# A dense fill sequence, second low-rank factors one pair earlier, and the RWKV output weights split during the first feed-forward stage

## The chip, the cores and the metric

The kernel runs on one core of one Trainium2 chip. The metric is the device time of one launch, in microseconds (us). The kernel before was run three times; the median is 1318.53 us, the lowest 1314.91 and the highest 1324.61.

A core has five engines that run beside each other, each with its own queue of instructions: PE (TensorE, matrix products), DVE (VectorE), ACT (ScalarE), POOL (GpSimd) and SP (SyncE, which here only starts DMAs). PEld is PE's loading of the stationary operand.

## The reference

The input is one sequence of 512 positions with 1024 channels, float32, and the model has two layers. Each layer adds a token mixer and then a gated feed-forward block to the residual, both behind an RMS norm, and one more RMS norm ends it.

```
layer 0:  h += sgu_mixer(norm(h))          # gated MLP with 128-position causal blocks
          h += conv_ffn(norm(h))           # (silu(gate) * val) @ w_down, FFN_DIM 2816
layer 1:  h += rwkv7_mixer(norm(h))        # 16 heads of 64, state 64x64 per head
          h += conv_ffn(norm(h))
return norm(h)

rwkv7_mixer:  xx = shift(h) - h;  x? = h + xx * mu[?]       for r, w, k, v, a, g
  r, k, v = xr @ w_r, xk @ w_k, xv @ w_v
  w = -softplus(-(w0 + tanh(xw @ w1) @ w2)) - 0.5;   a = sigmoid(a0 + (xa @ a1) @ a2)
  g = sigmoid(xg @ g1) @ g2
  S_t = S_{t-1} diag(exp(-exp(w_t))) + (S_{t-1} a_t) b_t^T + v_t k_t^T ;  y_t = S_t r_t
  return ((group_norm(y) + bonus) * g) @ w_o
```

## The kernel before, in words

**Matrix products.** Activations lie as eight tiles of 128 channels by 512 positions. Every float32 product is made of three fp32r matmuls: each operand is split into a high part (a cast on ACT, L213) and a low part (a subtraction, on DVE or POOL, L214), and `mm3` (L291 to L297) adds high times high, high times low and low times high. A tile of weights is loaded by one DMA from ACT's queue into `w32` (two buffers) and split into `wh` and `wl` (`WB` = 4 buffers each) by `weights`.

**Parts.** Splitting weights costs ACT and DVE time when the weights are used. For `w_k`, `w_v` and the first gate factor `g1`, `make_parts` therefore splits them early, beside the first feed-forward stage (`ffn` with l = 0): a step loads a piece of 128x512 from DRAM (SP, L253), splits the piece of the step before, and writes its two parts back to DRAM (SP, L257). The pieces have two buffers, each part one. In the stage's first loop (22 turns j, each two products of 24 matmuls) one step is taken per turn; in the second loop (8 output tiles) two per tile. With 35 pieces there are 36 steps. Later `parts` and `gate_parts` load the parts directly (L266, L272, L281, L282), with nothing left to split. The output weights `w_o` (`wo`) are not among them: `project` loads and splits them as it uses them, the second half of each load with its low part on POOL.

**The RWKV stage.** `rwkv_first` makes the low-rank hidden layer and r. `rwkv_main` then weaves three generators:

- *main*: `pairs` (eight pairs of heads; `decay`, `operands`, `products`), then two `scan`s over groups of eight heads, each eight chunks of 64 positions. A chunk is a chain in which PE (L1117, L1130, L1137, L1142) and DVE or ACT copies (L1119, L1131, L1132, L1140) wait for each other in turn.
- *side*: `invert`, which inverts the triangular blocks of a group, first on DVE (L964, L965, L970, L971), then with 32x32 matmuls on PE (L985, L988).
- *fill*: one long sequence of dense PE work, `projections` (k, then v; each v tile's `value` work, L784 and L798, is stepped in between as `late`), then `gates` (the gate's two factors), then `project` (the output product).

`weave` (L1258 on) advances main by one yield, adds `rate` to what fill is due, and takes that many steps of fill, whose PE instructions it puts behind the PE mark of `lag` yields earlier. The rates are RATES[0] and [1] for the pairs, [5] for their last two yields, [2] for the first scan, [3] for the second, [4] for the rest. LEAD is the number of fill steps taken between the end of the pairs and the first scan. Apart from such explicit orders the compiler's scheduler orders each engine's queue by its own estimate of when operands are ready.

**Where the changed parts act.** `second_factors` loads the second low-rank factors of two pairs (SP), and splits them (ACT L729, DVE L730) into `l2`, which has one set of buffers; `start` calls it when an even pair begins, and `decay` multiplies with it at once (L814, L816). In `projections`, the last `value` is drained step by step (`yield from late`). `gates` first loads its weights, yields once without PE work, and then per k mixes `x` (ACT L1010, DVE L1011, a split) and multiplies it at once with both columns of `g1`: six matmuls of 512 positions, three of them 32 columns wide. Two steps of the sigmoid follow, without PE work, then four `gate` steps that wait until the first scan's last block is normed. `project` takes two steps of six matmuls for each of 8 output tiles, once per group.

Of the kernel before, what the change touches and what calls it, by code (L numbers as in the profile page):

```python
# [28 lines left out]
GN_EPS = 64e-5  # L29
C1 = -0.5 * math.exp(-0.5)  # L30

RATES = ((1.9, 2), (1.9, 6, 2.2), (0.62, 2, 1), (0.85, 2), (2, 2), (0.7, 6, 2.2))
LEAD = 4
WB = 4
FIRST0, WAIT, STEPS = 1, 1, (2, 2, 2, 2, 2)
NKEY = 3
BT, SCAN = 1, 3
BANKS = ("mm", "aux", "e", "us")
PARTS = ("wk", "wv")


PARAMS = [
# [101 lines left out]
class Emit:  # L144
    def __init__(self, ctx, tc, A, out):
        self.tc, self.nc, self.A, self.out = tc, tc.nc, A, out
        nc = tc.nc
        self.gp = gp = ctx.enter_context(tc.tile_pool(name="gp", bufs=1))
        self.wp = ctx.enter_context(tc.tile_pool(name="wp", bufs=2))

        self.xr = ctx.enter_context(tc.tile_pool(name="xring", bufs=1))
        self.cst = gp.tile([P, NCST], F32, name="cst")
        self.par = gp.tile([P, NPAR], F32, name="par")

        self.hz = [gp.tile([P, T + 1], F32, name=f"h{k}") for k in range(KT)]
# [12 lines left out]

        dp = ctx.enter_context(tc.tile_pool(name="parts", bufs=1, space=DRAM))
        self.wd = {n: [dp.tile([P, 2, 1024], F32, name=f"{n}d{m}") for m in range(KT)] for n in PARTS}  # L170
        self.gd = dp.tile([P, 2, 1280], F32, name="g1d")
        self.n = self.turn = 0
        self.wq = nc.scalar
        self.ktiles = 2
        self.x = []
# [66 lines left out]
    def make_parts(self, pool):  # L242

        nc = self.nc
        at = [(self.A[n][m], self.wd[n][m], slice(c, c + 512)) for n in PARTS for m in range(KT) for c in (0, 512)]
        at += [(self.A["g1"], self.gd, slice(c, min(c + 512, 1280))) for c in (0, 512, 1024)]
        w = []
        for i in range(len(at) + 1):
            with self.tc.issue_after(self.last(mybir.EngineType.Activation)):
                if i < len(at):  # L250
                    src, _, c = at[i]
                    w.append(pool.tile([P, 512], F32, tag="pw", bufs=2, name=self.uid("pw"))[:, 0:c.stop - c.start])
                    nc.sync.dma_start(w[i], src[:, c])  # L253
                if i:
                    _, dst, c = at[i - 1]
                    for j, x in enumerate(self.split(pool, w[i - 1], [P, 512], "pw", bufs=1)):
                        nc.sync.dma_start(dst[:, j, c], x[:, 0:c.stop - c.start].bitcast(F32))  # L257
            yield
# [226 lines left out]
    def ffn(self, l, gain):  # L485
        nc, tc, A = self.nc, self.tc, self.A
        with ExitStack() as ctx:
# [11 lines left out]

            for j in range(NF):  # L500
                cv, accs = [], []
                next(parts, None)
                for i in (j, NF + j):
                    w = self.first if i == 0 else self.weights(A["wup"][l, i])
                    a = self.acc()
                    self.dense(a, w, x)
                    accs.append(a)
                    if i == 0:
                        norm = self.rstd()
                        next(norm)  # L510
# [12 lines left out]
                nc.vector.tensor_tensor(cv[1], cv[0], cv[1], ALU.mult)  # L523
                hid.append(self.split(fp, cv[1], [P, T], f"hid{j}"))
# [169 lines left out]
    def rwkv_main(self, r, ctx, gain):  # L694
# [13 lines left out]
        def tmp(tag, bufs, w=W2):  # L708
            return tile_([P, w], tag, bufs)
# [23 lines left out]
        def projections():  # L733
# [31 lines left out]
            late = iter(())  # L765
            for m in range(KT):
                a = self.acc("mm")
                for _ in self.dense_steps(a, load.take(), xv):
                    yield
                    next(late, None)  # L770
                for _ in late:
                    yield
                v = ip.tile([P, T], F32, tag="v", bufs=1, name=self.uid("v"))
                S.copy(v, a)
                late = value(m, v)
            yield from late

        def value(m, v):
            g, i = divmod(m, 4)
# [29 lines left out]
        def decay(p, u):  # L809
# [4 lines left out]
                nc.tensor.matmul(accs[j], l2[j][:, w], r.lr[j], start=True, stop=False)  # L814
            for j in range(2):
                nc.tensor.matmul(accs[j], l2[2][H[j], w], r.lr[j][H[j]], start=False, stop=True)  # L816
            th, u.ta = scratch("sq"), tmp("ta", 2, T)
            for j, x in enumerate((th, u.ta)):
                S.activation(x, accs[j], AF.Tanh, scale=0.5, bias=dq(j, p))
# [89 lines left out]
        def pairs():  # L909
# [3 lines left out]
            def start(p):  # L913
                if p >= KT:
                    return iter(())
                while p not in ks:
                    next(fill)
                if p % 2 == 0:
                    second_factors(p)
                return decay(p, units[p])  # L920

# [14 lines left out]
        def invert(g):  # L936
# [39 lines left out]
            for i in range(2):  # L976
                for hf in range(2):
# [17 lines left out]
                            S.copy(tg[b0, us, 32:64], ps[b0])  # L995
                    yield

        def gates():


            gw[0] = gate_weights(0)
            ws = self.gate_parts()
            yield
            accs = [self.acc("mm")[0:n] for n in (P, 32)]
            for k in range(KT):
                with ExitStack() as behind:
                    for eng in (mybir.EngineType.DVE, mybir.EngineType.Activation):
                        behind.enter_context(tc.issue_after(self.last(eng)))
                    j, t = 5 * KT + k, scratch("sq")
                    S.activation(t, self.hz[k][:, 0:T], AF.Copy, scale=self.p("mu", j))  # L1010
                    V.scalar_tensor_tensor(t, self.h[k], self.omu[:, j:j + 1], t, ALU.mult, ALU.add)  # L1011
                    x = self.operand(t)
                for a, w, n in zip(accs, ws, (P, 32)):
                    self.mm3(a, self.wcols(w, k * n, n), x, k == 0, k == KT - 1)
                yield
# [170 lines left out]
        def project():  # L1186

            def load(g, m):
                return self.weights(A["wo"][m:m + 2, :, 512 * g:512 * g + 512].rearrange("m p c -> p m c"), lo_eng=G)

            ws = Ahead([lambda g=g, m=m: load(g, m) for g in range(2) for m in range(0, KT, 2)] + [self.prefetch])
            def back(m):
# [128 lines left out]
```

## Time and profile before

| what | us |
|---|---|
| median of three runs | 1318.53 |
| the profiled execution, its own time | 1320.53 |
| its span, first to last instruction | 1318.7 |
| PE busy | 1275.4 |
| DVE busy | 852.3 |
| ACT busy | 631.1 |
| POOL busy | 141.5 |

The mean granted PE clock is 0.974 of full speed. All times of rows below are us from the start of the span. The RWKV stage's `rwkv_main` runs from about 570 to 945, the first scan from 758 to 833, the second until 902. A row of a stretch (A:B) gives each engine's busy time with its number of instructions, then the granted PE clock, the DMA engines' mean busy share, and GB/s. A row of a group gives its count, busy time and the mean nanoseconds of one, then the engine's idle time ahead of it and what ended that. A row of the timeline gives start, duration, the instruction, and in brackets the engine's idle time before it and what ended it.

### The profile page before, as it was taken

What the parts mean: (1) busy time and instruction counts of PE and PEld (TensorE: products, weight loads), DVE (VectorE), ACT (ScalarE), POOL (GpSimd) and SP (SyncE); (2) the same over time, 40 slices, a digit from 0 to 9 for tenths busy, and PEclk for the clock granted to TensorE, in tenths of its full rate; (3) what the DMA queues carried; (4) which work ended last, traced back from release to release, by engine and by line L of the source; (5) the groups of instructions that cost most, each with busy time, mean ns of one, the idle gap of its engine ahead of it and who ended that gap; (6) DMA issues with size and microseconds to landing.
All of it is one profiled execution on the core that took longest, in us unless ns stands there. A gap on an engine that the chain in (4) does not pass through costs nothing. (4 is left out here: it accounts for less than half of the span.)

```text
span 1318.7 us, 19468 instructions
## 1 busy us (share of the span) xinstructions
PE 1275.4 (97%) x7578; PEld 1025.9 (78%) x7578; DVE 852.3 (65%) x1371; ACT 631.1 (48%) x1072; POOL 141.5 (11%) x148
## 2 busy tenths in 40 slices
PE   8999999999999999999999998889999999999996
PEld 6878888888888888777777766567888888888886
DVE  5565487888775443847779584686687777772223
ACT  5444455555554333665675644443554445442221
POOL 3100200000000111211111022142300000000001
PEclk9999999999999999999899896899999999999998
DMA  7232345555556663237778695583322232223322
GB/s 258 89 112 81 109 149 171 167 166 174 170 175 213 218 204 109 81 121 202 204 215 259 165 222 123 128 223 105 96 96 96 96 96 96 96 92 97 95 88 76
DMA packets 101580, 189.06 MB, mean 143 GB/s; under 512 B 17072, under 2 KB 49072, under 8 KB 101488
## 3 DMA queue, kind: packets, MB, share of 16 engines
q10 hardware_dynamic: 36592, 109.46, 26.7%
q1 hardware_dynamic: 64896, 78.37, 20.7%
q8 instruction: 59, 0.97, 0.3%
q14 instruction: 33, 0.27, 0.1%
HBM read 146.63 MB, written 41.16 MB: 142 GB/s over the span
## 5 line engine op out<-in xcount | busy, mean ns | idle before, releaser
L213 ACT CAST wh<-w 128x512 fp32r<-128x512 f32 x356 | 217.0, 612 | 392.3 <-PE mm L296 104.4
L214 DVE TENSOR_TENSOR wl<-w,wh 128x512 fp32r<-128x512 f32 x348 | 239.6, 690 | 184.7 <-ACT wh L213 183.3
L295 PE MATMUL mm<-mxh,wh 128*128 128x512 f32 (+1 forms) x384 | 158.1, 412 | 1.4 <-DVE h L1208 1.3
L297 PE MATMUL mm<-mxh,wl 128*128 128x512 f32 (+1 forms) x384 | 152.7, 398 | 1.6 <-DVE wl L214 1.6
L296 PE MATMUL mm<-mxl,wh 128*128 128x512 f32 (+1 forms) x384 | 152.5, 397 | 0.0
L322 POOL TENSOR_TENSOR ss<-ss,sq 128x512 f32<-128x512 f32 x30 | 41.4, 1379 | 776.8 <-issue 594.8
L518 ACT ACTIVATE cv<-z,par 128x512 f32<-128x512 f32 x88 | 71.7, 817 | 36.1 <-DVE z L516 36.1
L295 PEld LDWEIGHTS mm<-mxh,wh 128*128 128x128 f32 (+1 forms) x384 | 72.7, 189 | 20.7 <-issue 3.4
L297 PEld LDWEIGHTS mm<-mxh,wl 128*128 128x128 f32 (+1 forms) x384 | 72.5, 189 | 19.4 <-DVE wl L214 2.6
L295 PE MATMUL e<-mxh,wh 128*128 128x512 f32 x216 | 84.7, 392 | 0.0
L296 PE MATMUL e<-mxl,wh 128*128 128x512 f32 x216 | 84.3, 390 | 0.0
L297 PE MATMUL e<-mxh,wl 128*128 128x512 f32 x216 | 84.3, 390 | 0.0
L296 PEld LDWEIGHTS mm<-mxl,wh 128*128 128x128 f32 (+1 forms) x384 | 72.9, 190 | 14.5 <-issue 0.5
L296 PE MATMUL aux<-mxl,wh 128*128 128x512 f32 x208 | 81.4, 391 | 1.5 <-POOL mxl L214 1.4
L295 PE MATMUL aux<-mxh,wh 128*128 128x512 f32 x208 | 81.5, 392 | 0.3 <-ACT mxh L213 0.3
L295 PE MATMUL us<-mxh,wh 128*128 128x512 f32 x208 | 81.5, 392 | 0.0
L519 DVE SCALAR_TENSOR_TENSOR cv<-z,par,cv 128x512 f32<-128x512 f32 x88 | 66.0, 751 | 23.9 <-ACT cv L518 23.9
L297 PE MATMUL aux<-mxh,wl 128*128 128x512 f32 x208 | 81.2, 391 | 0.0
L297 PE MATMUL us<-mxh,wl 128*128 128x512 f32 x208 | 81.2, 390 | 0.0
L296 PE MATMUL us<-mxl,wh 128*128 128x512 f32 x208 | 81.2, 390 | 0.0
L520 DVE SCALAR_TENSOR_TENSOR cv<-z,par,cv 128x512 f32<-128x512 f32 x88 | 66.0, 752 | 2.9
L295 PEld LDWEIGHTS e<-mxh,wh 128*128 128x128 f32 x216 | 40.6, 188 | 8.9 <-issue 0.5
(1092 smaller groups left out, 2713.3 us busy)
## 6 DMA issues: line engine op xcount, KB each, us to landing
w<-in_wup ACTq DMA_DIRECT2D x88, 512.0 KB, 3.6
w<-in_wdn ACTq DMA_DIRECT2D x32, 512.0 KB, 3.5
st<-std SPq DMA_DIRECT2D x30, 384.0 KB, 5.4
std<-lq SPq DMA_DIRECT2D x32, 256.0 KB, 4.3
w<-in_wdn ACTq DMA_DIRECT2D x16, 384.0 KB, 3.2
w<-in_wsu ACTq DMA_DIRECT2D x8, 512.0 KB, 3.6
w<-in_wso ACTq DMA_DIRECT2D x8, 512.0 KB, 3.5
pw<-in_wk SPq DMA_DIRECT2D x16, 256.0 KB, 3.7
```

The costliest lines, as they stand in the source:

```text
L213: nc.scalar.copy(hi[r, :n], src)
L214: (lo_eng or nc.vector).tensor_tensor(lo[r, :n], src, hi[r, :n].bitcast(F32), ALU.subtract)
L295: mm(acc, wh, xh, start=first, stop=False)
L296: mm(acc, wh, xl, start=False, stop=False)
L297: mm(acc, wl, xh, start=False, stop=last)
L322: nc.gpsimd.tensor_tensor(self.ss, self.ss, self.sq, ALU.add)
L518: nc.scalar.activation(c, z[:, 2:], AF.Identity, scale=cw(2, i), bias=self.p("conv_b", l * 44 + i))
L519: nc.vector.scalar_tensor_tensor(c, z[:, 1:T + 1], cw(1, i), c, ALU.mult, ALU.add)
L520: nc.vector.scalar_tensor_tensor(c, z[:, 0:T], cw(0, i), c, ALU.mult, ALU.add)
```

## The change

The second factors are made at the end of the odd pair before, gate operands two steps ahead of their use, the gate's weights at the last v tile; two yields of fill without dense work go; `wo` joins the weights split during the first feed-forward stage, with two steps of `make_parts` in each of the first 15 turns; and four rates and LEAD change.

```diff
-RATES = ((1.9, 2), (1.9, 6, 2.2), (0.62, 2, 1), (0.85, 2), (2, 2), (0.7, 6, 2.2))
-LEAD = 4
+RATES = ((1.9, 2), (1.9, 6, 2.2), (0.72, 2, 1), (0.72, 2), (2, 2), (1.2, 6, 2.2))
+LEAD = 1
...
-PARTS = ("wk", "wv")
+PARTS, LATER = ("wk", "wv"), ("wo",)
...
-        at = [(self.A[n][m], self.wd[n][m], slice(c, c + 512)) for n in PARTS for m in range(KT) for c in (0, 512)]
+        at = [(self.A[n][m], self.wd[n][m], slice(c, c + 512)) for n in PARTS + LATER for m in range(KT) for c in (0, 512)]
...
             for j in range(NF):
                 cv, accs = [], []
-                next(parts, None)
+                for _ in range(2 if j < 15 else 1):
+                    next(parts, None)
...
                 a = self.acc("mm")
-                for _ in self.dense_steps(a, load.take(), xv):
+                w = load.take()
+                if m == KT - 1:
+                    gw[0] = gate_weights(0)
+                for _ in self.dense_steps(a, w, xv):
                     yield
                     next(late, None)
+                    if m == KT - 1 and len(gx) < 2:
+                        gx.append(gate_mix(len(gx)))
...
-            yield from late
+            for _ in late:
+                pass
...
                 nc.tensor.matmul(accs[j], l2[2][H[j], w], r.lr[j][H[j]], start=False, stop=True)
+            if p % 2 == 1 and p + 1 < KT:
+                second_factors(p + 1)
...
-                if p % 2 == 0:
+                if p == 0:
                     second_factors(p)
...
+        gx = []
+
+        def gate_mix(k):
+            with ExitStack() as behind:
+                for eng in (mybir.EngineType.DVE, mybir.EngineType.Activation):
+                    behind.enter_context(tc.issue_after(self.last(eng)))
+                j, t = 5 * KT + k, scratch("sq")
+                S.activation(t, self.hz[k][:, 0:T], AF.Copy, scale=self.p("mu", j))
+                V.scalar_tensor_tensor(t, self.h[k], self.omu[:, j:j + 1], t, ALU.mult, ALU.add)
+                return self.operand(t)
+
         def gates():
-            gw[0] = gate_weights(0)
             ws = self.gate_parts()
-            yield
             accs = [self.acc("mm")[0:n] for n in (P, 32)]
             for k in range(KT):
-                with ExitStack() as behind:
...
-                    x = self.operand(t)
+                x = gx[k]
+                if k + 2 < KT:
+                    gx.append(gate_mix(k + 2))
...
             def load(g, m):
-                return self.weights(A["wo"][m:m + 2, :, 512 * g:512 * g + 512].rearrange("m p c -> p m c"), lo_eng=G)
+                t = []
+                for d in self.wd["wo"][m:m + 2]:
+                    x = tuple(self.wp.tile([P, 512], F32R, tag=tag, bufs=WB, name=self.uid(tag)) for tag in ("wh", "wl"))
+                    for i in range(2):
+                        self.wq.dma_start(x[i].bitcast(F32), d[:, i, 512 * g:512 * g + 512])
+                    t.append(x)
+                return 512, t
```

More of the change, by code (lines that the diff above doesn't have):

```diff
@@ L169, in __init__ @@
         dp = ctx.enter_context(tc.tile_pool(name="parts", bufs=1, space=DRAM))
-        self.wd = {n: [dp.tile([P, 2, 1024], F32, name=f"{n}d{m}") for m in range(KT)] for n in PARTS}
+        self.wd = {n: [dp.tile([P, 2, 1024], F32, name=f"{n}d{m}") for m in range(KT)] for n in PARTS + LATER}
         self.gd = dp.tile([P, 2, 1280], F32, name="g1d")
@@ L996, in invert @@
                     yield
+        gx = []
[7 more added lines that the diff above has]
+                return self.operand(t)
         def gates():
-            gw[0] = gate_weights(0)
             ws = self.gate_parts()
-            yield
             accs = [self.acc("mm")[0:n] for n in (P, 32)]
             for k in range(KT):
-                with ExitStack() as behind:
[L1007 to L1011, printed above, removed]
-                    x = self.operand(t)
+                x = gx[k]
+                if k + 2 < KT:
+                    gx.append(gate_mix(k + 2))
                 for a, w, n in zip(accs, ws, (P, 32)):
```

## The prediction

> **What bounds the kernel now.** I read the busy shares first, then the slices of the span, then stretches of the RWKV stage, then single waits of PE in the timeline.
>
> ```profile
> span 1318.7 us, 19468 instructions
> ...
> PE 1275.4 (97%) x7578; PEld 1025.9 (78%) x7578; DVE 852.3 (65%) x1371; ACT 631.1 (48%) x1072; POOL 141.5 (11%) x148
> ...
> PE   8999999999999999999999998889999999999996
> ...
> PEclk9999999999999999999899896899999999999998
> ```
>
> PE bounds the kernel: the other engines are far from full. What the change can return is therefore what PE loses, and both slice rows put that between slices 20 and 27, which is the RWKV stage. PE loses in two ways there: it idles, and its clock is granted at half. Stretches of that stage:
>
> ```profile
> 646.90:657.10 10.20, 10.20 (x56) 8.53 (x57) 5.02 (x10) 6.57 (x12) 1.40 (x2) 0.50 0.45 121
> 732.20:742.50 10.30, 10.30 (x98) 7.58 (x91) 2.74 (x4) 8.01 (x11) 0.00 (x0) 0.50 0.38 103
> 758.00:789.00 31.00, 29.18 (x384) 21.34 (x384) 27.39 (x68) 11.64 (x27) 5.86 (x7) 1.00 0.95 224
> 789.00:828.00 39.00, 32.29 (x568) 25.98 (x562) 20.85 (x44) 20.57 (x37) 9.08 (x12) 0.65 0.56 129
> 797.10:803.90 6.80, 5.58 (x70) 4.71 (x70) 3.69 (x9) 5.99 (x8) 3.17 (x3) 0.50 0.79 185
> 807.30:827.80 20.50, 19.53 (x348) 16.00 (x349) 7.86 (x15) 9.55 (x19) 4.67 (x7) 0.50 0.35 86
> 828.00:868.00 40.00, 35.02 (x416) 22.88 (x412) 26.36 (x56) 18.85 (x38) 8.82 (x9) 0.96 0.64 149
> 848.30:851.70 3.40, 3.40 (x21) 2.04 (x20) 0.75 (x1) 1.03 (x2) 0.00 (x0) 0.50 0.00 0
> 868.00:902.00 34.00, 31.67 (x374) 23.48 (x372) 24.04 (x50) 12.08 (x28) 13.02 (x12) 1.00 0.76 220
> 902.00:945.00 43.00, 40.83 (x206) 33.45 (x205) 28.86 (x44) 20.88 (x37) 15.66 (x15) 1.00 0.24 74
> ```
>
> After the five engines' columns comes the granted clock. The worst stretch is 789 to 828, the second half of the first scan: 39.00 - 32.29 = 6.7 us idle, and within it 27.3 us at half clock, in which PE was active 5.58 + 19.53 = 25.1 us; at full clock that work takes half, so 12.5 us are lost to the clock. The same rule gives 5.1 us lost at 647, 5.15 at 732 and 1.7 at 848.
>
> **The change part by part.** I count fill steps from the loops. Pairs yield 30 times; the key products need 38 calls, the v products 32 more. Five calls go before the first yield; 19 yields at 1.9 give 36, nine more 17, so 20 v steps are done when two yields of pairs are left.
>
> *D. The hole in the first scan (RATES[2], the two dropped yields, gate operands ahead).* Before, the two yields at 0.7 give 1 step and LEAD 4, so 25 v steps precede the scan, and its 24 yields at 0.62 give 14: seven v steps, two drains of the last value, one empty yield, four gate steps. The three poor calls come together, one per 1.6 yields. Here is what PE waits for there:
>
> ```profile
> 790.68 1.16 PE L784 MATMUL mm<-cst,v 128*128 128x128 f32 x8 [0.78 <-ACT v L774]
> ...
> 795.37 0.68 PE L1130 MATMUL us<-wt,ti 64*64 64x64 f32 x16 [1.34 <-DVE wt L1119]
> 797.55 0.47 PE L1142 MATMUL e<-vu,st 64*64 64x64 f32 x2 [1.50 <-DVE vu L1131]
> 798.79 1.12 PE L1137 MATMUL us<-vu,cbt 128*64 128x64 f32 x16 [0.77 <-ACT vu L1132]
> ...
> 807.36 1.12 PE L1137 MATMUL us<-vu,cbt 128*64 128x64 f32 x16 [1.40 <-ACT vu L1132]
> ...
> 814.80 0.80 PE L295 MATMUL mm<-mxh,w 128*128 128x512 f32 x1 [0.92 <-ACT mxh L213]
> ```
>
> These six waits are the 6.7 us: the scan's own chain of copies, with nothing dense to cover it, and at the end a gate product that waits for the operand mixed just ahead of it. After, the yields at 1.2 give 2 steps, LEAD 1, so 23 v steps precede the scan; 24 yields at 0.72 give 17: nine v steps, then all eight gate steps, of which the first also carries the last value. No call in the scan is without dense matmuls, and gate operands lie two steps ahead. I let one L1130 wait remain (1.34, taken as 1.5): -5.2. Of the clock, the inversion's 32x32 matmuls stay in this stretch, and with them some half clock; I take half of the 12.5 back, rounded to -6.5. Sum -11.7; ends -19.2 (all) and -3 (half the waits alone).
>
> *C. The end of the first inversion (RATES[5], LEAD).*
>
> ```profile
> 731.17 1.22 PE L985 MATMUL aux<-ix,ti 32*32 32x32 f32 x64 [1.62 <-DVE ix L970]
> ...
> 760.99 0.68 PE L1130 MATMUL us<-wt,ti 64*64 64x64 f32 x16 [1.27 <-DVE wt L1119]
> ```
>
> One more v step (six matmuls) falls into the pairs' last two yields, where PE waits 1.62 us, just ahead of the half clock at 732. A step outlasts the wait: -1.6, and half of the 5.15 us of clock, -2.5. Against it, three v steps fewer cover the start of the first scan, while DVE begins the second inversion; its first chunk waited 1.27 us before, and I let that come twice more, +2.5. Sum -1.6; ends -6.7 and +4.3.
>
> *B. Second factors one pair ahead.*
>
> ```profile
> 609.72 0.51 PE L814 MATMUL e<-lr,l 128*128 128x512 f32 x1 [0.82 <-ACT l L729]
> ...
> 645.28 0.49 PE L814 MATMUL e<-lr,l 128*128 128x512 f32 x1 [0.96 <-ACT l L729]
> ...
>   DMA w<-in_l: 6.7, 3
> ```
>
> Both waits of L814 (1.8 us) go; the last row, from the view of tile `l`, says that ACT itself stood 6.7 us, three times, for the factors' DMA. After, that DMA and the copies sit behind an odd pair's matmuls, and what stands behind them on ACT is that pair's tanh and, later, its square, for which PE waits; I put 1.0 us on that. The half clock at 647 follows the second wait; I take half of its 5.1 us. Sum -1.8 - 2.6 + 1.0 = -3.4; ends -6.9 and, if ACT's 6.7 us all reach PE, +4.9.
>
> *E. The second scan's start.* Its first calls are now the two sigmoid steps, which hold no matmul, then four small gate products, one call per 1.4 yields; before, gate steps 4 to 7 stood there.
>
> ```profile
> 838.51 0.51 PE L295 MATMUL mm<-mxh,w 128*128 128x512 f32 x1 [0.98 <-ACT mxh L213]
> ...
> 847.30 0.33 PE L1142 MATMUL e<-vu,st 64*64 64x64 f32 x2 [1.59 <-DVE vu L1131]
> ...
> 861.34 0.65 PE L1168 MATMUL aux<-cst,y 128*128 128x128 f32 x4 [0.46 <-DVE y L1164]
> ```
>
> All the idle time of 828 to 868 is 40.00 - 35.02 = 5.0 us, with 1.7 of clock: 6.7 that change hands. In its place the hole moves here, smaller: a chunk without fill waited 1.34 + 1.50 + 0.77 = 3.6 us, two stretches of half clock as at 797 cost 2.8, and of the gate's waits, 0.46 in the last row and its like, about 1.3 remain: 7.7. Sum +1.0; ends -5 and +8.
>
> *F. The output weights as parts.* Removed, from the groups of 850 to 945, are 16 of the casts, 8 DVE and 8 POOL subtractions; the other casts belong to the next stage.
>
> ```profile
> L213 ACT CAST wh<-w 128x512 fp32r<-128x512 f32 x22 | 13.2, 617 | 16.4 <-PE mm L296 6.6 <-DMA w<-in_wo 5.2 <-PE mm L297 2.5
> ...
> L214 POOL TENSOR_TENSOR wl<-w,wh 128x512 fp32r<-128x512 f32 x8 | 10.7, 1339 | 16.0 <-ACT wh L213 11.2 <-PE aux L1168 4.8
> ...
> 873.37 0.50 PE L297 MATMUL mm<-mxh,wl 128*128 128x512 f32 x1 [1.29 <-DVE wl L214]
> ...
> L272 ACTq DMA_DIRECT2D wh<-wvd x12: 326/326/1054, 664.4 to 744.4; - x12
> ...
> DMA to landing us min/median/max: 2.9/4.8/7.5
> ```
>
> That is 16 x 0.617 = 9.9 us of ACT and 10.7 of POOL, none of it on the path but the one wait of 1.29. Added are 32 DMAs in place of 8, on ACT's queue, 0.33 us each: four per load, which wait there until PE releases the buffers, ahead of the scan's copies. A load serves 24 matmuls; 206 in 43 us make that 5.0 us, and a buffer is released 1.5 loads before it is needed again, 7.5 us, against about 0.7 + 4.8 for issue and landing (rows of the v parts). So PE is fed: -1.3; ends -3 and, if the slowest landing of 7.5 came on three loads, 3 x 0.7 = 2 us, and as much behind ACT's queue, +4.
>
> *A. Sixteen more steps beside the first feed-forward stage.*
>
> ```profile
> 150.00:380.00 230.00, 230.00 (x1028) 190.72 (x1027) 177.27 (x267) 123.10 (x189) 2.88 (x6) 1.00 0.52 164
> ...
> 960.00:1190.00 230.00, 230.00 (x1015) 190.21 (x1014) 173.68 (x254) 112.71 (x169) 0.00 (x0) 1.00 0.31 98
> ...
> 250.57 0.43 SPq L253 DMA_DIRECT2D pw<-in_wk  x1
> ...
> 261.44 0.45 SPq L253 DMA_DIRECT2D pw<-in_wk  x1
> ...
> L214 DVE TENSOR_TENSOR pwl<-pw,pwh 128x512 fp32r<-128x512 f32 x19 | 13.0, 683 | 0.0
> ...
> wkd<-pwl SPq DMA_DIRECT2D x16, 256.0 KB, 3.3
> ...
> DMA to landing us min/median/max: 1.7/3.0/6.0
> ```
>
> The stage with parts and the second one without both show PE busy throughout, 1028 and 1015 matmuls in 230 us. A turn takes 10.9 us (the two issues). A second step adds 0.68 us to DVE, from 77% to about 83%, and 0.62 to ACT. The next step's low part waits until the last one's store has landed: 0.68 + 0.32 + 3.3 = 4.3 us per step, 8.6 for two, under 10.9. Cover: PE's own matmuls; +0.5, with the upper end in the second rival. The end of the stage keeps its spacing, two steps per tile.
>
> **Sum:** 0.5 - 3.4 - 1.6 - 11.7 + 1.0 - 1.3 = -16.5 us. The profiled execution took 1320.5 (its span and 1.8 us around it), 2.0 over the median, so the forecast is 1320.5 - 16.5 = 1304.0, and against the median 1302.0.
>
> **The rivals.**
>
> *First: the waits close, the clock does not.* The half clock would follow the kind of work, many small matmuls, and not the idle places. For it: at 807 to 828 the clock is half with PE busy 19.53 of 20.50 us, and the 348 instructions there stay. Against it: half clock begins right behind waits at 647, 732, 797, and the dense 902 to 945 has none despite 2.2 us of idle. Without the clock terms (6.5, 2.5, 2.6 and E's -1.7 + 2.8) the sum is -16.5 + 11.6 - 1.1 = -6.0: 1312.5 against the median. [...]
>
> *Second, slower: the parts' chain binds the first loop.* Its place is the 15 turns with two steps; its price is twice (0.68 + 0.32 + landing) above a turn's 10.9 us. It binds from a landing of 4.45 us. At 5.0 it costs 15 x 1.1 = 16.5 us and eats the gain; at 6.0, the longest row, 15 x 3.1 = 46.5, for 1302 + 46 = 1348. For it: the DMA share is 0.52 with one step, 0.31 without, so about 0.73 with two. Against it: the median is 3.0, and tiles with two steps already run without PE idling.
>
> *Third: time given back.* The hole returns at its old size in the second scan: E at +8 and D's clock untouched, -16.5 + 7 + 6.5 = -3: 1315.5. For it: sigmoid steps hold no matmul. Against it: they make one chunk poor, where 1.6 were.
>
> *Fourth: the order does not change much,* because the scheduler places by its own estimates: 1318.5. Against it: the count of seven v steps in the first scan fits what PE ran there.
>
> **How the numbers follow.** Forecast 0.52, between 1291 and 1309; first rival 0.24; second 0.10; third 0.09; fourth 0.05. For 8 in 10, I go down to 1290 (D whole, other terms as taken) and up to 1320 (the first, third and fourth rivals, and the second up to its break-even). A measurement here tells about 1% (13 us) from no change. Faster by over 1% (below 1305.3) is most of the forecast and a little of the first rival, 0.50; slower by over 1% (above 1331.7) is most of the second rival and mishaps of C and F, 0.08; the rest 0.42.
>
> **What would show it.** Right: between 789 and 828 dense matmuls in every few us, the six waits down to one or two, and less half clock; L814 without waits on ACT; no casts of output weights after 850; 150 to 380 with PE busy throughout. Wrong: half clock as long as before (first rival), PE idle or waits for low parts in the first loop (second), new waits and half clock behind the start of the second scan (third), or ACT standing in front of L1132 for its own DMAs.

## The result, and the profile after

The changed kernel takes 1308.72 us (median of 17 runs, 1303.88 to 1319.56) against 1318.48 (17 runs, 1311.78 to 1324.61) for the kernel before beside it: ratio 0.9922, 95% interval 0.9903 to 0.9941, a gain of 9.8 us or 0.8%: in the forecast's direction, and 6.7 us above the 1302.0 of the forecast. The profiled execution took 1305.46 us, 15.1 less than the profiled one before. The page after, the same rows as before (in after's code the scan's lines are 14 higher, L814 is L821, L970 is L979):

```profile
span 1303.7 us, 19609 instructions
...
PE 1262.6 (97%) x7578; PEld 1015.2 (78%) x7578; DVE 852.5 (65%) x1379; ACT 627.9 (48%) x1072; POOL 129.9 (10%) x140
...
PE   8999999999999999999999988999999999999996
...
PEclk9999999999999999999999899999999999999998
```

PE has the same 7578 matmuls and is still the bound. The row PE dips in two slices where it dipped in three; the row PEclk has one dip left of four, the last slice aside, and the 6 is gone. To place the gain I cut the RWKV stage at the same places of the program: from the start of the low-rank stage to the first scan, the first scan, and the second scan with the output up to the second feed-forward stage. Windows of the kernel before, then of the kernel after (length; busy time of PE, PEld, DVE, ACT, POOL; clock; DMA share; GB/s):

```profile
584.60:758.10 173.50, 167.64 (x1373) 128.28 (x1371) 126.31 (x230) 109.88 (x205) 24.29 (x25) 0.93 0.72 206
758.10:832.30 74.20, 65.67 (x983) 49.90 (x983) 50.91 (x117) 33.42 (x66) 14.94 (x19) 0.82 0.73 170
832.30:943.70 111.40, 101.92 (x944) 75.92 (x940) 76.48 (x141) 50.05 (x98) 37.49 (x35) 0.98 0.52 142
```

```profile
585.20:747.90 162.70, 156.96 (x1363) 119.75 (x1361) 125.70 (x227) 108.33 (x203) 22.51 (x23) 0.98 0.75 215
747.90:824.90 77.00, 68.88 (x1011) 48.88 (x1010) 57.79 (x129) 40.52 (x78) 17.03 (x21) 0.98 0.82 196
824.90:928.60 103.70, 97.47 (x924) 76.35 (x924) 61.30 (x124) 35.14 (x73) 25.30 (x27) 0.95 0.68 179
```

The three stretches together go from 359.1 to 343.4 us: -15.7, so the whole difference lies here. The single stretches can't be set one against one, since fill work was moved into the first scan (983 matmuls become 1011). Idle time of PE (length less busy) falls little: 5.9 + 8.5 + 9.5 = 23.9 before, 5.7 + 8.1 + 6.2 = 20.1 after, -3.8. Time at half clock, 2 x (1 - clock) x length, falls from 24 + 27 + 4 = 55 to 7 + 3 + 10 = 20 us. In the kernel after, dense matmuls start 0.43 us apart at half clock (L295 to L297 at 732.11, 732.54 and 732.97) and 0.23 at full clock (721.64, 721.87 and 722.11): while PE is active, about half of a stretch at half clock is lost, so this is where most of the 15.7 lie.

The clock also differs between runs of one kernel, and that separates the profile's -15.1 from the median's -9.8. After's 17 runs follow their mean clock closely: at 0.989 a run takes about 1305, at 0.977 1319.6. I take span x (1 - clock) as the clock's loss at most: an estimate from the halved pace above, which counts PE's idle time at half clock too (1.22 of the 6.80 us at 797 before). Averaged over the 83 runs of the kernel before that stand beside the experiments, and over after's 17, it is 29.9 us before and 20.2 after, and what is left of the time is 1289.9 before and 1288.7 after. **Of the means' gain of 10.8 us, up to ten are clock and one is all else.** The profiled run after (0.989, mean 0.9845) had luck, the one before (0.974, mean 0.977) was a little worse than the average.

In the scan's stretch of 789 to 828, the rows of after (windows, then the chain's waits of PE in 747.9 to 824.9: total us, times, longest):

```profile
780.00:815.00 35.00, 31.01 (x565) 21.98 (x566) 24.39 (x53) 22.18 (x40) 6.29 (x9) 1.00 0.78 185
789.00:828.00 39.00, 34.99 (x630) 24.57 (x626) 25.71 (x51) 25.28 (x47) 8.73 (x10) 1.00 0.63 147
```

```profile
PE us L1144 <- DVE wt L1133: 2.6, 3, 1.8
PE mm L805 <- ACT vt L796: 1.8, 1, 1.8
PE aux L994 <- issue: 1.4, 1, 1.4
PE us L1144 <- issue: 1.3, 1, 1.3
```

The clock is full where it was 0.65. The waits are not gone: the scan moved some ten microseconds earlier, and in the like stretch PE idles 35.00 - 31.01 = 4.0 us where it idled 6.7; over the whole first scan 8.1 against 8.5. They are in part other waits than the six before: two of PE's pauses in the middle of groups of small matmuls ("issue"), and one of 1.8 us for the value's copy on ACT.

### The profile page after: what moved, and what is told of

Same layout as the page of the kernel before. It is cut to its first block, busy times and chain, and to the rows that moved or that the text cites. A ratio compares the mean times of both kernels' runs of the same rounds, so it can differ in the third digit from the quotient of the medians.

```text
span 1303.7 us, 19609 instructions
## 1 busy us (share of the span) xinstructions
PE 1262.6 (97%) x7578; PEld 1015.2 (78%) x7578; DVE 852.5 (65%) x1379; ACT 627.9 (48%) x1072; POOL 129.9 (10%) x140
## 4 chain that ended last, share of the span: by engine, by line
PE 78%; DVE 8%; issue 3%; DMA 3%; ACT 2%; POOL 1%; SPq 0%; ACTq 0%; DVEq 0%; POOLq 0%
PE mm L295 8%; PE mm L297 8%; PE mm L296 8%; PE aux L295 6%; PE aux L296 6%; PE aux L297 6%; PE us L297 5%; PE us L295 5%; PE us L296 5%; PE e L297 5%; PE e L296 5%; PE e L295 5%; DVE pr L973 1%; DVE tt L974 1%; DVE lq L900 1%
## 5 line engine op out<-in xcount | busy, mean ns | idle before, releaser
L213 ACT CAST wh<-w 128x512 fp32r<-128x512 f32 x340 | 206.3, 610 | 344.9 <-PE mm L296 87.7
L214 DVE TENSOR_TENSOR wl<-w,wh 128x512 fp32r<-128x512 f32 x340 | 232.0, 684 | 179.7 <-ACT wh L213 178.2
L295 PE MATMUL mm<-mxh,wh 128*128 128x512 f32 (+1 forms) x384 | 156.9, 409 | 0.0
L297 PE MATMUL mm<-mxh,wl 128*128 128x512 f32 (+1 forms) x384 | 153.2, 399 | 0.3 <-DVE wl L214 0.3
L295 PEld LDWEIGHTS mm<-mxh,wh 128*128 128x128 f32 (+1 forms) x384 | 72.4, 188 | 18.0 <-issue 2.6
L297 PEld LDWEIGHTS mm<-mxh,wl 128*128 128x128 f32 (+1 forms) x384 | 72.4, 189 | 17.6 <-DVE wl L214 0.8
L295 PE MATMUL e<-mxh,wh 128*128 128x512 f32 x216 | 84.5, 391 | 0.0
L297 PE MATMUL e<-mxh,wl 128*128 128x512 f32 x216 | 84.1, 389 | 0.0
L295 PE MATMUL aux<-mxh,wh 128*128 128x512 f32 x208 | 81.5, 392 | 0.3 <-ACT mxh L213 0.3
L295 PE MATMUL us<-mxh,wh 128*128 128x512 f32 x208 | 81.2, 391 | 0.0
L297 PE MATMUL aux<-mxh,wl 128*128 128x512 f32 x208 | 81.0, 390 | 0.0
L297 PE MATMUL us<-mxh,wl 128*128 128x512 f32 x208 | 81.0, 389 | 0.0
L296 PEld LDWEIGHTS aux<-mxl,wh 128*128 128x128 f32 x208 | 39.1, 188 | 12.3 <-POOL mxl L214 2.7
```

Of the source, the lines that this page charges most:

```text
L213: nc.scalar.copy(hi[r, :n], src)
L214: (lo_eng or nc.vector).tensor_tensor(lo[r, :n], src, hi[r, :n].bitcast(F32), ALU.subtract)
L295: mm(acc, wh, xh, start=first, stop=False)
L296: mm(acc, wh, xl, start=False, stop=False)
L297: mm(acc, wl, xh, start=False, stop=last)
```

## The experiments

The theory at this point (T1 in the expectations): the gain is the clock in the first scan, and what buys it is that the fill's new order leaves no call there without dense matmuls. Two other theories stand beside it in the expectations: T2 has the gain from ACT, DVE and POOL being relieved of the output weights' splits, T3 from the second factors. The rivals are those of the prediction. Each kernel is either the changed one with one part undone, or the kernel before with one part (once two) alone, or one of the two with something added. The ratios compare with runs of the kernel before on the same chip: 1319.85 (29 runs) for the four kernels with a part undone, 1317.85 (35) for the three with one part alone and for the kernel before with dense matmuls added, 1319.5 (19) for the other four. Intervals are about 0.3% to each side, 4 us; smaller differences between two kernels aren't told apart.

### The fill's order

Undone in the changed kernel (gate weights, gate operands and the two empty yields as before):

```diff
-                w = load.take()
-                if m == KT - 1:
-                    gw[0] = gate_weights(0)
...
-            for _ in late:
-                pass
+            yield from late
...
+            gw[0] = gate_weights(0)
+            yield
...
-                x = gx[k]
-                if k + 2 < KT:
-                    gx.append(gate_mix(k + 2))
```

> The changed kernel with the fill sequence of before (last value drained by yields, empty yield, gate operands mixed just ahead of their product); rates, factors and output weights as changed. Theory 1: the poor calls are back, 23 v steps before the scan and 17 calls in it give 9 v steps, 3 poor calls and 5 gate steps, so the half clock comes back in part: 1313 to 1318, clock 0.972 to 0.981. Theory 2 and 3: no loss, 1307 to 1311.

Alone, on the kernel before (the same lines the other way round):

> The kernel before with the new fill sequence alone (last value drained at once, no empty yield, gate operands two ahead, gate weights at the last v tile). Theory 1: undoing this part cost the clock about 0.004, so it gains that alone: 1313 to 1317, clock 0.979 to 0.983. If the parts only work together: 1318 to 1321.

Undone it took 1312.21 us, 0.9940 (0.9916 to 0.9964), between what the theories expected; alone 1316.57, 0.9979 (0.9953 to 1.0005). The first scan's stretch for the order undone; then the first and the second scan for the order alone:

```profile
750.20:830.40 80.20, 69.67 (x980) 51.62 (x979) 51.29 (x118) 33.62 (x66) 16.56 (x21) 0.83 0.77 188
```

```profile
759.10:830.00 70.90, 64.91 (x991) 47.01 (x990) 56.02 (x125) 38.21 (x74) 15.48 (x19) 0.93 0.75 175
830.00:940.90 110.90, 101.31 (x931) 78.09 (x931) 71.44 (x134) 44.93 (x90) 37.81 (x35) 0.92 0.52 145
```

The first scan's clock follows the order: 0.83 without it, as in the kernel before (0.82), 0.93 with it alone. The time follows less: the order alone shortens that scan from 74.2 to 70.9 us, and its median gains 1.3 us, within its interval of no change. In its second scan the clock is 0.92 where the kernel before has 0.98, so what the first scan wins back the second loses, and over its runs the mean clock stays at 0.978, below the 0.979 to 0.983 expected.

### Dense matmuls that do nothing else

The kernel before with six dense matmuls in each of its three poor calls (two drains, one empty yield). This parts T1 from the first rival, by which the many small matmuls themselves hold the clock down: they all stay.

```diff
+        def warm(x, n=6):
+            a = self.acc("mm")
+            for i in range(n):
+                nc.tensor.matmul(a, x[0][:, 0:P], x[0], start=i == 0, stop=i == n - 1)
...
-            yield from late
+            r.warm = xv[KT - 1]
+            for _ in late:
+                warm(r.warm)
+                yield
...
+            warm(r.warm)
             yield
```

> The kernel before, with six extra dense matmuls (128x128 by 128x512, result unused) added to each of its three poor fill calls in the first scan: the two drains of the last v tile and the empty yield. It computes the same and does about 4 us more PE work (18 matmuls of 0.23 us), and changes nothing else. Theory 1 (the clock falls where dense work is missing): most of this work falls into the 6.7 us of waits, and the mean clock rises from 0.977 by 0.004 or more, so 1311 to 1316 where the kernel before takes 1319. The first rival of the prediction (the half clock follows the small matmuls, which stay): the clock stays at 0.977 and the time rises by up to 4 us, 1319 to 1323.

1315.60 us, 0.9980 (0.9952 to 1.0009). The first scan:

```profile
753.00:825.10 72.10, 66.87 (x1003) 49.17 (x1002) 50.81 (x117) 33.33 (x66) 14.99 (x19) 0.91 0.76 175
```

With more work the scan is shorter: half clock 2 x 0.09 x 72.1 = 13 us in place of 27. Over the runs the clock's loss falls by 8.2 us (29.5 to 21.3), and the rest grows by 5.6, for the added matmuls (about 4 us) and what they push. The first rival, that the small matmuls by themselves hold the clock down, is refuted: the same small matmuls run at a higher clock when dense ones stand between (0.91 in this profile, 0.82 in that of the kernel before). This kernel doesn't part thin work from idle places, since PE's idle time in the scan falls too, from 8.5 to 5.2 us; the changed kernel does, in part: there it is 8.1 us at a clock of 0.98.

### The rates

`RATES` and `LEAD` of before in the changed kernel, and those of after in the kernel before:

```diff
-RATES = ((1.9, 2), (1.9, 6, 2.2), (0.72, 2, 1), (0.72, 2), (2, 2), (1.2, 6, 2.2))
-LEAD = 1
+RATES = ((1.9, 2), (1.9, 6, 2.2), (0.62, 2, 1), (0.85, 2), (2, 2), (0.7, 6, 2.2))
+LEAD = 4
```

> The changed kernel with the four rates and LEAD of before; everything else changed. Theory 1 (the gain is PE clock won back by dense fill in the first scan): with 0.62 and LEAD 4 only 14 calls fall into the first scan and 25 v steps ahead of it, but none of the 14 is poor any more, so about half of the 9.8 us is lost: 1312 to 1316, with a mean clock between 0.975 and 0.983. Theory 2 (the gain comes from ACT, DVE and POOL being relieved of the output weights' splits): no loss, 1307 to 1311. Theory 3 (it is the second factors): no loss either.

> The kernel before with the four rates and LEAD of the changed one alone. Three poor calls stay in the first scan, one per 1.4 yields, so they fill a shorter stretch, and more dense calls follow them in it. Theory 1: a little gain, 1315 to 1319. The prediction's term C alone: 1.6 us of gain, 1317.

Undone, 1309.95 (0.9920, 0.9887 to 0.9952): no loss, where a loss was expected. Alone, 1315.74 (0.9976, 0.9949 to 1.0004). The first scan, of the rates undone, then of the rates alone:

```profile
752.00:823.60 71.60, 64.43 (x991) 46.54 (x990) 56.24 (x125) 38.33 (x74) 15.47 (x19) 0.95 0.85 194
758.40:836.20 77.80, 68.01 (x980) 50.75 (x979) 51.30 (x118) 33.67 (x66) 16.60 (x21) 0.85 0.72 173
```

The rates don't mend the clock there (0.85); the order does it without them (0.95).

### Order and rates together, without the output's parts

> The kernel before with the new fill sequence and the new rates and LEAD, without the second factors' move and without the output weights' parts. Alone the two gained 1.3 and 2.1 us against a kernel before of 1317.9. If they work together (the sequence has no poor call, the rates bring dense calls to the place): the half clock of the first scan goes and the time is 1311 to 1315, clock 0.981 to 0.985. If they only add up: 1314 to 1317. Without the output weights as parts, casts that wait for their DMA should stand ahead of the scan's copies in the second scan, with waits of PE for ACT there.

1318.06 us, 0.9994 (0.9966 to 1.0023): nothing of a gain shows, against both expectations. The two scans, and PE's waits in the second:

```profile
749.80:826.10 76.30, 69.91 (x1011) 49.26 (x1010) 57.43 (x129) 40.52 (x78) 17.42 (x21) 0.96 0.75 177
826.10:936.20 110.10, 98.69 (x925) 76.94 (x924) 70.59 (x132) 44.01 (x89) 36.25 (x35) 0.94 0.55 143
```

```profile
PE us L1148 <- ACT vu L1143: 6.2, 3, 5.3
PE aux L1179 <- DVE y L1175: 3.0, 1, 3.0
```

The first scan is as good as after's (0.96), and the second pays: PE idles 110.10 - 98.69 = 11.4 us there (9.5 before, 6.2 after), 9.2 of it for the scan's copy on ACT and for y, and its clock is 0.94. This is the prediction's third rival, time given back in the second scan; what keeps it out of the changed kernel is the part that follows. The rows are of one of its quickest executions, though, 1312.51 us: over the 12 runs the mean clock is 0.9785 against 0.9775 before, so most runs lose more of it than this profile, and where they do isn't shown.

### The output's weights

Undone in the changed kernel (loaded whole and split beside the second scan, one step of parts per turn), and alone on the kernel before:

```diff
-PARTS, LATER = ("wk", "wv"), ("wo",)
+PARTS, LATER = ("wk", "wv"), ()
...
-                for _ in range(2 if j < 15 else 1):
-                    next(parts, None)
+                next(parts, None)
...
-                for d in self.wd["wo"][m:m + 2]:
...
+                return self.weights(A["wo"][m:m + 2, :, 512 * g:512 * g + 512].rearrange("m p c -> p m c"), lo_eng=G)
```

> The changed kernel with the output weights loaded and split where they are used, as before, and one step of parts per turn in the first feed-forward stage. By the prediction's term F it loses 1.3 us and by A gains 0.5: 1308 to 1311. Theory 1: the same. Theory 2: it loses most of the gain, 1315 or more.

> The kernel before with the output weights as parts alone (two steps per turn for 15 turns, direct loads in the output product). Undoing it took back 5 us of the changed kernel's gain, against the prediction's F of 1.3. If that stands for itself: 1313 to 1317. By the prediction's F and A: 1317 to 1319. By the second rival (the parts' chain binds): 1325 or more.

Undone, 1314.30 us (0.9953, 0.9927 to 0.9978): 5.6 above the changed kernel's median, 4.1 by the two ratios, which is at the edge of what is told apart, and the largest loss of any part. Alone, 1311.59 (0.9945, 0.9919 to 0.9971): 6.3 of gain, the only part whose own interval excludes no change. Both lie outside what was expected. The second scan with the output, undone, then alone:

```profile
828.20:937.50 109.30, 97.21 (x925) 75.67 (x924) 70.69 (x132) 43.94 (x89) 36.26 (x35) 0.95 0.54 144
```

```profile
826.70:934.60 107.90, 102.02 (x942) 76.38 (x939) 67.48 (x133) 41.13 (x81) 25.34 (x27) 0.98 0.64 172
```

Where the weights stay whole, PE idles 12.1 us; with the parts alone 5.9, against 9.5 before. What PE waits for, and what ACT, DVE and PE do just then, all of the kernel with the part undone (waits of PE in 828 to 945; the timelines of ACT, of DVE and of PE):

```profile
PE us L1150 <- ACT vu L1145: 6.2, 3, 3.9
PE aux L1181 <- DVE y L1177: 3.7, 2, 3.0
```

```profile
850.63 0.62 ACT L213 CAST wh<-w 128x512 fp32r<-128x512 f32 x1 [4.48 <-DMA w<-in_wo]
851.15 0.61 ACT L213 CAST gwh<-w 128x512 fp32r<-128x512 f32 x1
851.67 0.61 ACT L225 CAST gw<-w 32x512 fp32r<-32x512 f32 x1
852.30 0.37 ACT L1145 COPY vu<-us 64x256 f32<-64x256 f32 x1
```

```profile
846.79 0.41 DVE L1144 COPY vu<-us 64x256 f32<-64x256 f32 x1
```

```profile
852.73 1.12 PE L1150 MATMUL us<-vu,cbt 128*64 128x64 f32 x16 [3.92 <-ACT vu L1145]
```

L1144 and L1145 copy the two halves of one PE result. DVE took its half at 846.79; ACT took the other at 852.30, although its operand had been there as long. In between, a cast of the output's weights stood on ACT 4.48 us for its DMA, and two casts of the gate's weights followed: ACT kept to the order of its queue. For this copy of 0.37 us the scan's next matmuls wait: PE idles 3.92 us and comes back at half clock (0.82 over 852.70 to 866.40), with 1.12 us for 16 such matmuls where the group before it at 841.47 took 0.69. The longest wait of the kernel with order and rates alone, 5.3 us, is for the same copy on ACT (L1143 there). The grouped row of L213 (prediction, F) shows this only as idle time of the casts, 5.2 us of it behind "DMA w<-in_wo"; ACT's timeline puts the two side by side.

In the kernel before, the same weights cost PE waits of another kind in the second scan (832 to 945):

```profile
PE mm L297 <- DVE wl L214: 1.3, 1, 1.3
PE mm L295 <- DVE h L1208: 1.3, 2, 0.9
...
PE us L1117 <- DVE vu L1140: 0.9, 1, 0.9
```

With the parts alone all three are gone, together 3.5 us, as much as the stretch is shorter (111.4 to 107.9). The median gains 6.3; 2.8 us of that I can't place. Over the runs, span x (1 - clock) falls from 29.5 to 25.4 us and the rest of the time by 2.1, so a part of the gain may be clock; not in the first scan, whose clock in this kernel's profile is as low as before (0.81).

### The second factors

Made at the start of an even pair again:

```diff
-            if p % 2 == 1 and p + 1 < KT:
-                second_factors(p + 1)
...
-                if p == 0:
+                if p % 2 == 0:
```

> The changed kernel with the second factors made when an even pair begins, as before. By the prediction's term B it loses 3.4 us: 1312. Theory 1, after seeing that both waits of the low-rank matmuls on the factors' cast are still there in the changed kernel (0.73 and 0.97 us, with the factors' DMA issued at the same moment as before): no loss, 1307 to 1311. Theory 3: it loses most of the gain, 1315 or more.

1311.55 us, 0.9931 (0.9900 to 0.9961): not told apart from the changed kernel. Why the early place doesn't help shows in the changed kernel's own rows: PE's waits in 570 to 740 and SP's queue in 600 to 650. Then the issues of the factors' DMA, after, and last before:

```profile
PE e L821 <- ACT l L730: 1.7, 2, 1.0
```

```profile
SPq L729 <- PE mm L296: 8.8, 1, 8.8
```

```profile
605.01 0.82 SPq L729 DMA_DIRECT2D w<-in_l  x2
...
641.01 1.07 SPq L729 DMA_DIRECT2D w<-in_l  x2
```

```profile
604.59 0.82 SPq L728 DMA_DIRECT2D w<-in_l  x2
...
641.08 1.06 SPq L728 DMA_DIRECT2D w<-in_l  x2
```

The call was moved a pair ahead in the program and the DMA was issued at the same moments. At 605 the reason shows: it needs a buffer of the ring w32, which the key's weights hold until PE is through with them (8.8 us in SP's queue). At 641 SP waits only 0.5 us for PE, behind other waits in its queue, so there the reason is open. Hence a kernel that loads the factors into a buffer of the operands' ring:

```diff
-            w32 = self.wp.tile([P, 1024], F32, tag="w32", bufs=2, name=self.uid("w32"))
+            w32 = self.xr.tile([P, T], F32, tag="mxl", bufs=10, name=self.uid("l32"))
...
-                w = w32[:, 512 * j:512 * j + 2 * P]
+                w = w32[:, 256 * j:256 * j + 2 * P]
```

> The changed kernel with the second factors loaded into a buffer of the operand ring in place of one of the two weight buffers w32. In the changed kernel their DMA is issued when w32 comes free (605.0 and 641.0 us), as before the change, and the low-rank matmuls wait 0.73 and 0.97 us for their cast. Theory 1: with a buffer of its own the DMA goes early, both waits go, and the time falls by at most 1.7 us plus what half clock follows them: 1303 to 1309. If the DMA is held by something else, the two waits stay and the time is 1307 to 1311.

1311.18 us, 0.9926 (0.9894 to 0.9957): not told apart from the changed kernel. L821 waits no more, and this came in its place (waits of PE, then ACT's timeline):

```profile
PE e L845 <- ACT sq L835: 6.3, 2, 5.5
```

```profile
665.75 0.40 ACT L730 CAST l<-l 128x256 fp32r<-128x256 f32 x1 [3.93 <-DMA l<-in_l]
666.06 0.62 ACT L835 ACTIVATE sq<-kn 128x512 f32<-128x512 f32 x1
```

ACT stands 3.93 us for the factors' DMA with the pair's square behind it, and PE waits 5.46 us for the square. It is ACT's order once more. The borrowed buffers are the operands' own, so some of this may be their ring's; what is shown is that freeing the DMA alone isn't enough.

### Parts at three steps per turn

```diff
-                for _ in range(2 if j < 15 else 1):
+                for _ in range(3):
```

> The changed kernel with three steps of parts per turn in the first feed-forward stage until all are made. By the prediction's second rival a step takes 4.3 us and three take 12.9, over a turn's 10.9: were the chain to bind PE, the 17 turns would cost 17 x 2.0 = 34 us, 1340 or more. Theory 1: the steps' engines only lag and PE keeps its weights, so 1306 to 1312.

1357.99 us, 1.0294 (1.0254 to 1.0333). The first feed-forward stage of the changed kernel, then of this one; then PE's and ACT's waits of this one there:

```profile
150.00:380.00 230.00, 230.00 (x1028) 190.72 (x1027) 185.89 (x283) 128.75 (x204) 2.88 (x6) 1.00 0.69 215
```

```profile
150.00:380.00 230.00, 201.47 (x842) 155.23 (x841) 154.10 (x237) 106.83 (x177) 2.88 (x6) 0.99 0.73 232
```

```profile
PE mm L295 <- ACT wh L213: 8.0, 5, 2.1
PE us L297 <- DVE wl L214: 8.0, 8, 1.3
```

```profile
ACT pwh L213 <- DMA wod<-pwh: 27.9, 11, 5.1
ACT pwh L213 <- DMA wkd<-pwh: 24.9, 9, 4.7
ACT pwh L213 <- DMA wvd<-pwh: 16.6, 8, 4.9
```

At two steps a turn PE doesn't idle for one of the 230 us. At three, 28.5 us: ACT's next high part waits until the last one's store has landed, the stage's own casts wait behind it, and PE for those. That is the second rival's mechanism, one step beyond the change: three steps of 4.3 us don't fit 10.9 us. The prediction has the low part wait for the store; here it is ACT's high part, which holds up more, and the cost of 49 us is above the 34 expected.

### Dense matmuls at the second scan's start

Six such matmuls in each of the changed kernel's two sigmoid steps, which hold none:

```diff
+                warm(x)
```

> The changed kernel with six extra dense matmuls (result unused, 1.4 us each time) in each of the two sigmoid steps at the start of the second scan. The prediction's term E has a hole there with half clock. If that hole costs clock: the clock rises by 0.002 or more and the time falls to 1304 to 1308. If it does not (in the profile of the changed kernel the half clock at that place is 3.4 us): the time rises by 1 to 3 us, 1309 to 1312.

1306.93 us, 0.9909 (0.9873 to 0.9945). The interval holds the changed kernel's 0.9922; whether the hole still costs something stays open. The second scan's clock is 1.00 in this profile, and also in those of two kernels without these matmuls, the factors undone and the factors in the other ring.

## Why the prediction was right, and where not

- **What bounds it, and the sum.** Right: the whole difference lies in PE's losses in the RWKV stage. -9.8 came for -16.5, inside the range. That the sum came this near is in part luck: B and C, -5.0 together, brought nothing that the rows show, and F brought about as much more than its -1.3.
- **A, +0.5.** Right: 230.00 of 230, 1028 matmuls in both. DVE is at 185.89 / 230 = 81% (83 expected), the DMA share 0.69 (0.73).
- **B, -3.4.** The step "both waits of L814 go" failed: 1.7 us remain of 1.8, since the DMA starts when it did before, in one of the two cases because a buffer, not the place in the program, sets the moment. What I put at 1.0 us, the square behind the factors on ACT, is what one gets when the buffer is free (6.3). "The half clock at 647 follows the second wait" doesn't hold in every run: of four profiles of that same stretch of program, two (before, and the order alone, which differs only later) have 24 us at half clock (3.4 us of them at 671, which the prediction leaves out), and two have 14 and run at full clock at 647 to 657, behind the same wait of 0.98 us. So 2.6 us were taken from one profile. The two with 14 are the kernel with the added dense matmuls, whose rows follow, and the one with the output's parts alone (also 0.96):

```profile
644.57 0.50 PE L823 MATMUL e<-lr,l 128*128 128x512 f32 x1 [0.98 <-ACT l L729]
```

```profile
583.80:753.00 169.20, 163.20 (x1375) 124.39 (x1374) 126.28 (x230) 109.73 (x205) 24.21 (x25) 0.96 0.75 211
```

```profile
646.90:657.10 10.20, 10.20 (x80) 7.57 (x77) 9.25 (x14) 7.12 (x14) 3.09 (x3) 1.00 0.57 165
```

- **C, -1.6.** "A step outlasts the wait" failed; the wait is there as before:

```profile
725.23 1.20 PE L994 MATMUL aux<-ix,ti 32*32 32x32 f32 x64 [1.64 <-DVE ix L979]
```

```profile
725.50:735.80 10.30, 10.30 (x159) 7.42 (x153) 3.51 (x4) 8.01 (x11) 0.00 (x0) 0.67 0.44 120
```

  Half clock follows it again, for 2 x 0.33 x 10.30 = 6.8 us where it was 10.3; that it is shorter can't be put down to the rates, since over the whole stretch up to the first scan they point both ways: with the rates alone the clock is 0.91, below the 0.93 before, and with them undone 0.96, below the 0.98 after. The last dense matmuls ahead of this wait end at 722.7 us, before it begins, and none stands beside it: more fill in a call doesn't cover a wait that comes behind the fill.
- **D, -11.7.** The term was mis-sized in both its parts, in opposite ways. The waits (-5.2) fell by 0.4 in the scan as a whole. The clock (-6.5, half of 12.5 taken) came back for the most part: half clock in the scan goes from 27 to 3 us in this profile, and in those of the other eight kernels with the new order it is 0 to 16 us, 7 in the middle. By its cause it was right: the first scan's clock is 0.81 to 0.85 in the four profiles with the old order and nothing added, and 0.90 to 1.00 in all nine with the new one; the added matmuls lift it to 0.91 in the old order.
- **E, +1.0.** The mechanism was right and the sign depended on F: with the casts in place the second scan idles 11.4 us, without them 6.2, less than the 9.5 before. Its clock says the same: 0.92 to 0.95 in the three profiles with the new order and the casts, 0.95 to 1.00 in the six with the new order and the parts, 0.97 or 0.98 in the old order.
- **F, -1.3.** The most mis-sized term: -6.3 alone, and 5.6 lost when undone (4.1 by the ratios). The step that failed is "none of it on the path but the one wait of 1.29". I asked where PE waits for a low part; it also waits for what stands behind the casts and subtractions on their engines: h and vu on DVE before, and vu on ACT, behind casts that stand for a DMA, once the first scan is mended.
- **The rivals.** By the time alone 1308.72 lies nearer to the first rival's 1312.5 than to the forecast's 1302.0; the rows part them, and there the rival has its opposite: the clock came, the waits stayed. The second isn't in the change but one step from it: 1357.99 at three steps, 49 us over 1308.72. The third shows in the rows where order and rates go without the output's parts. The fourth is refuted by the first scan's clock.
- **Open.** The parts don't add up: order and rates together gain 1.4 us, the output's parts 6.3, all together 9.8, and differences of 4 us aren't told apart. How much of the 9.8 is whose is not settled beyond this: the order mends the first scan's clock, and with the parts the second scan doesn't lose it again. Nor are the second factors settled: the kernel with the output's parts undone and the one with order and rates alone differ in nothing else that acts, and 0.9953 against 0.9994 is at the edge of what is told apart. Also open are the two waits marked "issue" of 1.44 and 1.30 us in the middle of groups of small matmuls.

## What to carry to other kernels

Where an engine takes its work in order, as ACT did here, price a cast that waits for a DMA by what stands behind it, not by its own duration: 4.5 us of waiting and a copy of 0.4 made 3.9 us of idle PE. Moving a load earlier in the program did nothing where a buffer decided when it starts (issued at 605.01 us, and at 604.59 before); look for the queue's own wait first. And when fill work is moved into a hole, look at where it was taken from: the same hole opened one scan later (PE idle 11.4 us there, 9.5 before), until the casts there were gone too (6.2).

## What the runs showed of the hardware

**Half clock came in stretches of 3.4 us and whole multiples of it.** The stretches of the kernel before whose rows show a clock of 0.50 are 3.40, 6.80, 10.20, 10.30 and 20.50 us long, within 0.1 us one, two, three, three and six times 3.4. In the same kernel, of 40 windows of 0.5 us from 640 to 660, 38 show 1.00 or 0.50, and the other two (0.89 and 0.87) hold the edges of the stretch at 647 to 657. How much there is differs between profiles of one program: 24 us of half clock in two profiles of a stretch and 14 in two others; and the runs of one kernel took 1303.9 to 1319.6 us, with mean clocks from 0.989 to 0.977. No run shows what decides it.

**The clock fell behind waits of 1.64 us and less.** No wait between 700 and the half clock at 728 of the changed kernel is over 1.64 us, and in the kernel before it lasted 20.50 us from 807 on, with PE busy 19.53. What makes it fall isn't shown by such waits alone: behind one of 0.98 us at 644 two profiles ran on at full clock. How much dense work keeps the clock was not measured: 18 dense matmuls spread over three calls took the first scan's half clock from 27 to 13 us in one profile, and the loss of the whole kernel from 29.5 to 21.3 us over the runs.
